# The MLP of a two-layer decoder: the norm's factor, squared, applied once to the sum of three or four down quarters instead of to every up chunk

## The chip, the cores and the metric

The kernel runs on one core of a Trainium2 chip. The metric is device time in microseconds (us) of one execution. Shapes in profile rows are partitions x elements. PE is the matrix engine (TensorE), DVE is VectorE, ACT is ScalarE, POOL is GpSimd, SP is the engine whose queue issues nearly all DMAs. DVE and ACT each work off one queue in the order in which the program stands.

## The reference

The whole program is two decoder layers on 512 tokens of width 1024, then a final norm. The change is in the MLP that ends each layer:

```python
def rmsnorm(x, g):
    xf = x.astype(jnp.float32)
    y = xf * lax.rsqrt(jnp.mean(xf * xf, axis=-1, keepdims=True) + EPS)
    return (y * g.astype(jnp.float32)).astype(x.dtype)

def hybrid_layer(...):
    ...                                   # attention, retention, gates
    x = x + mixed @ w_out
    h2 = rmsnorm(x, g_mlp)
    x = x + jnp.square(jax.nn.relu(h2 @ w_up)) @ w_down
    return x
```

`w_up` is 1024 x 4096 and `w_down` 4096 x 1024. The norm's factor is one number r for each token, and relu is positively homogeneous, so relu(r·u)² = r²·relu(u)². The factor can therefore be applied to the 4096 up channels, or, squared, to the 1024 columns that come out of `w_down`.

## The kernel before, in words

Everything lies transposed: channels on the 128 partitions, the 512 tokens along the free axis. `x` holds 8 chunks of 128 channels. All products are made in three passes to keep float32 accuracy: each operand is split into a high part (`hi`, rounded by ACT) and a low part (`lo`, the rest, by DVE), and PE adds hi·hi, hi·lo and lo·hi.

Weights stream through SP's queue, 512 KB at a time, in an order written out by hand (`unit_order`). `split_until` turns each raw unit into `hi` (ACT, L286) and `lo` (DVE, L287), three units ahead of their use; the tiles of `raw`, `hi` and `lo` have three buffers each.

The MLP works in four quarters q = 0..3 of 1024 up channels. The order is in `mlp_sequence`: first the four up chunks 0 to 3 (`group`), then pairs of up chunks, written here as pair (q, i), with i = 0..3, chunk number c = 8q + 2i; between two pairs stands a "down" step (q, i), which multiplies quarter q's up result with two column chunks of `w_down` (`two_chunks`: 48 products 512 wide). So down (q, i) and pair (q+1, i) alternate, until the last quarter's down follows in one piece: in layer 0 as a `group` of four chunks and four single ones, in layer 1 in `end`.

A pair is computed in Winograd's form: seven products of half blocks instead of eight, into three PSUM banks called `a`, `b` and `e`. The order on PE is a; e; b; a; b; e; b, four steps of k each. `narrow_pair` makes each step of three products 256 wide; `wide_pair` of one product 512 wide (both moving parts side by side) and one 256 wide, and then has to fold the two halves of a bank together. Pairs with a chunk number from `FIRST_WIDE` = 6 on are wide. Between the products the banks are handed on:

```python
ins = ... nc.scalar.activation(b, a, AF.Copy).ins       # b starts as a copy of a        (L1383)
multiply(e, part, False, form(0))
ins = nc.scalar.activation(eu, e, AF.Copy).ins          # e saved                        (L1386)
multiply(b, part, True, form(1), False)
ins = nc.scalar.activation(bu, b, AF.Copy).ins          # b saved, before b goes on      (L1390)
```

PE's next products into `b` wait for the copy from `a`, and its products with `form(2)` wait until `b` has been saved. At its end the pair's `z` is joined from the banks (L1362, L1363, L1367 to L1369), multiplied with the factor and clipped by DVE (L1409), squared by ACT (L1429) and split (L339, L340) into quarter q's moving operand.

The factor comes from `rms_mlp`: the squares of `x` are summed while `x` is finished (`squared_input`), and `prepare` and `finish` run inside the first up group. A down step's two banks are added to `x` by DVE (L1436). With the last quarter of layer 0, `x` also goes to DRAM (`spill`) and is split as the next layer's input; in layer 1 the two halves of `x` are turned from channels to tokens by way of DRAM (`turns`: `blocks`, L520 and L523), the first half during the last down steps of quarter 2.

Tile's scheduler sets the order of the instructions on each engine when the program is built, from an estimate of their times. The order is fixed from then on.

## Time and profile before

| | |
|---|---|
| three runs | 1468.44, 1469.42, 1469.47 us; median 1469.42 |
| profiled execution, first to last instruction | 1467.5 us (1.9 less than the median: what lies around the span) |
| PE busy | 1461.0 us, 100% |
| DVE busy | 1161.6 us, 79% |
| ACT busy | 814.6 us, 56% |
| moved by DMA | 198.65 MB, 135 GB/s on average |

The profile has one row for each kind of instruction, with the number of times it ran, its busy time and the mean of one. A row of the timeline has start, duration, engine, line, what is written and read, and, in brackets, how long the engine had been idle and who ended that. Two neighbours on one engine overlap a little, so durations add up to somewhat more than the time between starts.

### The profile page before, as it was taken

The numbers are of one execution on the slowest core, as the hardware profiler recorded it, in microseconds if no ns is written. First come the engines' busy times: TensorE is split into PE (matmuls) and PEld (weight loads), VectorE is DVE, ScalarE is ACT, GpSimd is POOL, SyncE is SP. The second block draws the span as 40 slices with busy tenths as digits, with TensorE's granted clock in tenths as the row PEclk, the third lists the DMA queues.
The fourth block names the chain that finished last, engine by engine and source line by source line (L and its number), as shares of the span: only waits on it lengthen the run. The fifth ranks groups of instructions, "written<-read, shape, count | busy, mean of one in ns | idle before, by whom it ended". The sixth has DMA issues, their size and how long they took to land.

```text
span 1467.5 us, 20166 instructions
## 1 busy us (share of the span) xinstructions
PE 1461.0 (100%) x7434; PEld 1246.4 (85%) x7434; DVE 1161.6 (79%) x1912; ACT 814.6 (56%) x1306; POOL 3.7 (0%) x14
## 2 busy tenths in 40 slices
PE   9999999999999999999999999999999999999998
PEld 7888888888988888888888888888989888888887
DVE  7998778678988787776678977786899877877774
ACT  7657356654684445444456653666547754455544
POOL 0000000000000000000000000000000000000000
PEclk9999999999999999999999999999999999999999
DMA  6423843356443332333543258323654432333373
GB/s 227 134 87 101 280 166 98 104 171 210 130 120 125 101 115 88 107 108 115 165 121 102 86 168 285 107 95 107 191 197 123 144 101 87 125 105 101 108 200 108
DMA packets 73346, 198.65 MB, mean 135 GB/s; under 512 B 8712, under 2 KB 8864, under 8 KB 73248
## 3 DMA queue, kind: packets, MB, share of 16 engines
q1 hardware_dynamic: 72960, 196.84, 42.5%
q8 instruction: 58, 0.95, 0.3%
q10 hardware_dynamic: 288, 0.52, 0.1%
q14 instruction: 40, 0.33, 0.1%
HBM read 173.73 MB, written 20.98 MB: 133 GB/s over the span
## 4 chain that ended last, share of the span: by engine, by line
PE 99%; DVE 0%; issue 0%; POOLq 0%; ACT 0%; DVEq 0%; ACTq 0%
PE mm L334 24%; PE mm L332 23%; PE mm L333 23%; PE mm L1356 11%; PE mm L1357 6%; PE rv L332 2%; PE rv L334 2%; PE rv L333 2%; PE score L864 1%; PE r L332 1%; PE r L334 1%; PE r L333 1%; PE pT L819 0%; PE pv L846 0%; PE pv L845 0%; PE warm L311 0%
## 5 line engine op out<-in xcount | busy, mean ns | idle before, releaser
L333 PE MATMUL mm<-r,hi 128*128 128x512 f32 (+1 forms) x1568 | 572.5, 367 | 0.0
L332 PE MATMUL mm<-r,hi 128*128 128x512 f32 (+1 forms) x1568 | 569.9, 367 | 0.0
L334 PE MATMUL mm<-r,lo 128*128 128x512 f32 (+1 forms) x1568 | 563.9, 367 | 0.2
L286 ACT ACTIVATE hi<-raw 128x1024 fp32r<-128x1024 f32 (+1 forms) x334 | 333.9, 1002 | 377.8 <-PE mm L333 206.9
L287 DVE TENSOR_TENSOR lo<-raw,hi 128x512 fp32r<-128x512 f32 (+1 forms) x335 | 384.3, 1150 | 110.8 <-ACT hi L286 109.4
L334 PEld LDWEIGHTS mm<-r,lo 128*128 128x128 f32 x1568 | 293.6, 188 | 48.8 <-DVE lo L287 1.4
L332 PEld LDWEIGHTS mm<-r,hi 128*128 128x128 f32 x1568 | 294.1, 188 | 46.5 <-ACT r L342 0.2
L333 PEld LDWEIGHTS mm<-r,hi 128*128 128x128 f32 x1568 | 294.3, 188 | 46.0
L1356 PE MATMUL mm<-r,hi 128*128 128x512 f32 x728 | 252.0, 391 | 0.0
L1357 PE MATMUL mm<-r,lo 128*128 128x256 f32 x728 | 200.3, 277 | 0.0
L1356 PEld LDWEIGHTS mm<-r,hi 128*128 128x128 f32 x728 | 136.5, 188 | 28.7 <-ACT mm L1383 0.2
L1357 PEld LDWEIGHTS mm<-r,lo 128*128 128x128 f32 x728 | 136.7, 188 | 3.2 <-DVE lo L287 0.6
L1429 ACT ACTIVATE z<-z 128x512 f32<-128x512 f32 x56 | 32.5, 624 | 51.8 <-DVE z L1409 51.8
L1436 DVE TENSOR_TENSOR x<-x,mm 128x512 f32<-128x512 f32 x56 | 37.7, 686 | 28.1 <-PE mm L334 28.1
L334 PE MATMUL rv<-hi,r 128*128 128x512 f32 x128 | 49.8, 389 | 0.0
L333 PE MATMUL rv<-lo,r 128*128 128x512 f32 x128 | 49.8, 389 | 0.0
L332 PE MATMUL rv<-hi,r 128*128 128x512 f32 x128 | 49.8, 390 | 0.0
L339 ACT ACTIVATE r<-z 128x512 fp32r<-128x512 f32 x64 | 38.5, 619 | 16.3 <-DVE z L1090 16.1
L340 DVE TENSOR_TENSOR r<-z,r 128x512 fp32r<-128x512 f32 x64 | 42.9, 685 | 4.7 <-ACT r L339 4.3
L891 ACT ACTIVATE sm<-sm,st 128x256 f32<-128x256 f32 (+1 forms) x64 | 30.1, 472 | 19.0 <-DVE st L879 18.8
L1409 DVE SCALAR_TENSOR_TENSOR z<-z,rstd 128x512 f32<-128x512 f32 x52 | 35.6, 685 | 0.6
L340 DVE TENSOR_TENSOR r<-sums,r 128x1024 fp32r<-128x1024 f32 x24 | 28.9, 1216 | 0.0
(270 smaller groups left out, 1679.2 us busy)
## 6 DMA issues: line engine op xcount, KB each, us to landing
raw<-w_in_in SPq DMA_DIRECT2D x89, 512.0 KB, 3.6
raw<-w_down_in SPq DMA_DIRECT2D x64, 512.0 KB, 3.6
raw<-w_up_in SPq DMA_DIRECT2D x32, 512.0 KB, 3.9
raw<-w_up_in SPq DMA_DIRECT2D x60, 256.0 KB, 2.9
raw<-w_a_in SPq DMA_DIRECT2D x8, 512.0 KB, 6.5
ahead<-w_b_in SPq DMA_DIRECT2D x8, 512.0 KB, 5.4
park_w_b<-ahead SPq DMA_DIRECT2D x16, 256.0 KB, 5.9
ahead<-w_up_in SPq DMA_DIRECT2D x8, 512.0 KB, 5.7
```

Of the source, the lines that this page charges most:

```text
L286: nc.scalar.activation(hi[:, at], raw[:, at], AF.Copy)
L287: last_low[:] = [nc.vector.tensor_tensor(lo[:, at], raw[:, at], f32(hi[:, at]), ALU.subtract).ins]
L332: nc.tensor.matmul(ps, ah, bh, start=start and i == 0, stop=False, **more)
L333: nc.tensor.matmul(ps, ah, bl, start=False, stop=False, **more)
L334: nc.tensor.matmul(ps, al, bh, start=False, stop=stop and i == n - 1, **more)
L339: nc.scalar.activation(hi, src, AF.Copy)
L340: nc.vector.tensor_tensor(lo, src, f32(hi), ALU.subtract)
L1356: nc.tensor.matmul(both, hi[:, c], m, start=start and k == 0, stop=False, **more)
L1357: nc.tensor.matmul(ps[:, :H], lo[:, c], m[:, 0, :], start=False, stop=k == 3 and start, **more)
L1409: nc.vector.scalar_tensor_tensor(z[:, :, at], z[:, :, at], 0.0, factor, ALU.max, ALU.mult)
L1429: nc.scalar.activation(z[:, i, :], z[:, i, :], AF.Square)
L1436: nc.vector.tensor_tensor(x[:, c, :], x[:, c, :], ps, ALU.add)
```

## The change

The up chunks no longer carry the factor. Each is only clipped, squared and split. The squared factor, 1/(mean + eps), is applied once to the sum of the down quarters: in layer 0 to the sum of all four (`plain` = 4), in layer 1 to the sum of the first three (`plain` = 3), after which the last quarter's pairs carry the plain factor (`root`) as before. In detail:

- Layer input: when a chunk of `x` is final after `w_out`, it is stored to DRAM (`kept`, 8 stores of 256 KB for each layer) and not squared then. The squares are taken in the first up group, in its last two steps.
- Down quarter 0 is copied into `x` by ACT (L1440). Each further quarter starts with `x` copied into its two PSUM banks by ACT (`seed`, L1429), the products are added on top of it, and the result is copied back by ACT. At the last plain quarter DVE multiplies the bank with the squared factor and adds the old `x`, which comes back from `kept` (4 loads of 512 KB for each layer, `kept_pair`).
- `FIRST_WIDE` is 4, so pair (0, 2) is wide too.
- In `wide_pair`, `b` is no longer saved to `bu` but copied into bank `e` (L1384), onto which the later products of `e` are added; the two halves of `eu` are folded once, and one add of each join falls away. Relu and square are done by ACT on 1024 elements at once, and the split too.
- `finish` of the factor comes after down (0, 0), without a square root; layer 1 takes one root for its last quarter.

```diff
-FIRST_WIDE, LAST_WIDE = 6, 32
+FIRST_WIDE, LAST_WIDE = 4, 32
...
         def next_input(c):
             scaled_input(c, g_mlp)
-            squared_input(c, g_mlp)
+            nc.sync.dma_start(kept[:, c, :], x[:, c, :])
...
             def join_copied(dest, ps, u):
-                nc.vector.tensor_tensor(u[:, :H], u[:, :H], u[:, H:], ALU.add)
-                nc.vector.tensor_tensor(u[:, :H], u[:, :H], ps[:, H:], ALU.add)
-                nc.vector.tensor_tensor(dest, ps[:, :H], u[:, :H], ALU.add)
+                side = temp("side")[:, :H]
+                nc.vector.tensor_tensor(side, ps[:, H:], u, ALU.add)
+                nc.vector.tensor_tensor(dest, ps[:, :H], side, ALU.add)
...
             multiply(b, part, True, form(1), False)
-            ins = nc.scalar.activation(bu, b, AF.Copy).ins
+            nc.vector.tensor_tensor(u, u, eu[:, H:], ALU.add)
+            ins = nc.scalar.activation(e, b, AF.Copy).ins
...
-            for half in (1, 0):
-                ...
-                nc.vector.scalar_tensor_tensor(z[:, :, at], z[:, :, at], 0.0, factor, ALU.max, ALU.mult)
+            join(z[:, 1, :H], b)
+            if q < plain:
+                nc.scalar.activation(z, z, AF.Relu)
+            else:
+                factor = roots[0].unsqueeze(1).broadcast_to([P, 2, T])
+                nc.vector.scalar_tensor_tensor(z, z, 0.0, factor, ALU.max, ALU.mult)
...
-            for i in range(2):
-                nc.scalar.activation(z[:, i, :], z[:, i, :], AF.Square)
-                split(hi[:, i, :], lo[:, i, :], z[:, i, :])
+            nc.scalar.activation(z, z, AF.Square)
+            split(hi, lo, z)
...
+        def seed(c):
+            ps = bank(ps_mm, "mm")
+            nc.scalar.activation(ps, x[:, c, :], AF.Copy)
+            return ps
+        def kept_pair(c):
+            two = big("kept")
+            nc.sync.dma_start(two, kept[:, c : c + 2, :])
+            return two
+        def put_down(c, q, old=None):
             def put(ps):
-                nc.vector.tensor_tensor(x[:, c, :], x[:, c, :], ps, ALU.add)
+                if q < plain - 1:
+                    nc.scalar.activation(x[:, c, :], ps, AF.Copy)
+                    return
+                t = temp("down")
+                nc.vector.tensor_tensor(t, ps, rms_mlp.value, ALU.mult)
+                nc.vector.tensor_tensor(x[:, c, :], t, old[:, c % 2, :], ALU.add)
...
+                old = kept_pair(2 * i) if q == plain - 1 else None
+                seeded = [seed(c) for c in (2 * i, 2 * i + 1)] if q else None
+                two_chunks("w_down", layer, up[q], [put_down(c, q, old) for c in (2 * i, 2 * i + 1)], turning, seeded)
+                if (q, i) == (0, 0):
+                    rms_mlp.finish()
```

The scheduler builds a new order from this. Counted over both layers, PE has 112 products 256 wide less and 56 products 512 wide more; ACT has 57 instructions more (40 seeds, 40 copies back, and larger ones in place of smaller), DVE 126 fewer, SP 24 DMAs more.

**ACT, where pair (1, 2) of layer 0 begins.** `z` is the pair before, (1, 1); `mm` are PSUM banks, `side` and `eu` parts of the joins, `hi<-raw` the weights. Before:

```order
L286 ACTIVATE hi<-raw_4563 128x1024
L1362 ACTIVATE side<-mm 128x256
L1429 ACTIVATE z<-z 128x512 x2
L339 ACTIVATE r_87<-z 128x512
L286 ACTIVATE hi<-raw_4658 128x1024
L339 ACTIVATE r_87<-z 128x512
L1383 ACTIVATE mm<-mm 128x512
L286 ACTIVATE hi<-raw 128x512
L1386 ACTIVATE eu<-mm 128x512
L1390 ACTIVATE bu<-mm 128x512
```

Now, in the same place (L1376 is what was L1383, L1384 what was L1390):

```order
L1359 ACTIVATE side<-mm 128x256
L1400 ACTIVATE z<-z 128x1024
L1422 ACTIVATE z<-z 128x1024
L1440 ACTIVATE x<-mm 128x512
L339 ACTIVATE r_87<-z 128x1024
L286 ACTIVATE hi<-raw_4632 128x1024
L1440 ACTIVATE x<-mm 128x512
L1376 ACTIVATE mm<-mm 128x512
L286 ACTIVATE hi<-raw 128x512
L1379 ACTIVATE eu<-mm 128x512
L1384 ACTIVATE mm<-mm 128x512
```

The copy of bank `a` to bank `b` used to stand behind squares, splits and a weight conversion alone, none of which needs the last down step. It now stands behind two copies of down banks to `x` as well, which do, and between those two stand the split of `z` and the weight conversion.

**ACT, from pair (0, 3) to down (0, 0) and pair (1, 0) of layer 0.** Here `r_89` is the high part of pair (0, 3), which down (0, 0) multiplies with, `rstd<-own` the factor's four copies. Before:

```order
L286 ACTIVATE hi<-raw_4210 128x1024
L1362 ACTIVATE side<-mm 128x256
L1383 ACTIVATE mm<-mm 128x512
L286 ACTIVATE hi<-raw_4305 128x1024
L1386 ACTIVATE eu<-mm 128x512
L1429 ACTIVATE z<-z 128x512 x2
L1390 ACTIVATE bu<-mm 128x512
L339 ACTIVATE r_89<-z 128x512
L286 ACTIVATE hi<-raw 128x512
L339 ACTIVATE r_89<-z 128x512
```

Now:

```order
L286 ACTIVATE hi<-raw_4186 128x1024
L1359 ACTIVATE side<-mm 128x256
L1400 ACTIVATE z<-z 128x1024
L1376 ACTIVATE mm<-mm 128x512
L1422 ACTIVATE z<-z 128x1024
L472 ACTIVATE rstd<-own 64x256 x4
L286 ACTIVATE hi<-raw_4288 128x1024
L1379 ACTIVATE eu<-mm 128x512
L339 ACTIVATE r_89<-z 128x1024
L286 ACTIVATE hi<-raw 128x512
L1359 ACTIVATE side<-mm 128x256
L1384 ACTIVATE mm<-mm 128x512
```

Relu and square of `z`, the four copies of the factor and a weight conversion now stand ahead of the split into `r_89`, and the bank copy L1384 stands behind that split.

**SP, at the last down step of quarter 2 in layer 1**, where half of `x` is turned. Before:

```order
L225 DMA raw<-w_up_in 128x1024
L196 DMA raw<-w_down_in 128x1024
L520 DMA blocks<-turned 128x512 x2
L523 DMA x<-blocks 32x4x512 x4
L196 DMA raw<-w_down_in 128x1024 x4
```

Now:

```order
L225 DMA raw<-w_up_in 128x1024
L196 DMA raw<-w_down_in 128x1024
L520 DMA blocks<-turned 128x512 x2
L523 DMA x<-blocks 32x4x512 x4
L1434 DMA kept<-kept 128x1024
L196 DMA raw<-w_down_in 128x1024 x4
```

The last load of the old `x` stands behind the four loads of the turned blocks, which wait for their stores.

## The prediction

> **What bounds the kernel now.** I read the page's first parts, then the chain, then who makes PE wait.

> ```profile
> span 1467.5 us, 20166 instructions
> PE 1461.0 (100%) x7434; PEld 1246.4 (85%) x7434; DVE 1161.6 (79%) x1912; ACT 814.6 (56%) x1306; POOL 3.7 (0%) x14
> PEclk9999999999999999999999999999999999999999
> PE 99%; DVE 0%; issue 0%; POOLq 0%; ACT 0%; DVEq 0%; ACTq 0%
> PE warm L311 <- DVE ones L306: 1.0, 1, 1.0
> ```

> PE is busy all the time at full clock; the chain that ended last is PE itself, and the waits of PE hold one row, at the program's start. So a microsecond that DVE saves is worth nothing unless PE waited for it, and time can change in two ways only: PE gets other products, or PE begins to wait. DVE is the fuller of the helpers (79%), ACT has 44% free. But free share is no cover by itself: PE waits for particular ACT instructions, and those for what stands ahead of them in ACT's queue. So I price the products first and then walk ACT's and SP's queue at the places shown above.

> **Products.** A row's duration overlaps its neighbour, so the price of a product is the distance of starts.

> ```profile
> 423.96 0.28 PE L332 MATMUL mm<-r,hi 128*128 128x256 f32 x1
> 430.32 0.28 PE L332 MATMUL mm<-r,hi 128*128 128x256 f32 x1
> ...
> 513.78 0.39 PE L333 MATMUL mm<-r,hi 128*128 128x512 f32 x1
> 515.36 0.39 PE L334 MATMUL mm<-r,lo 128*128 128x512 f32 x1
> 516.27 0.40 PE L1356 MATMUL mm<-r,hi 128*128 128x512 f32 x1
> 517.53 0.28 PE L1357 MATMUL mm<-r,lo 128*128 128x256 f32 x1
> 520.70 0.39 PE L1356 MATMUL mm<-r,hi 128*128 128x512 f32 x1
> ```

> Narrow: from 423.96 to 430.32 lie 54 products, 0.118 us each. Down: 513.78 to 515.36 are 7, 0.226 each. Wide: 516.27 to 520.70 are 13 couples of 512 and 256, 0.341 each. A narrow pair has 84 products, 9.89 us; a wide one 28 couples, 9.55. Pair (0, 2) going wide saves 0.34 in each layer: **−0.7 us**. The extra product that clears a bank is there once a layer before and after.

> **What the helpers are given.** These are the prices on ACT and DVE, from the groups by shape:

> ```profile
> L286 ACT ACTIVATE hi<-raw 128x1024 fp32r<-128x1024 f32 x291 | 307.3, 1057 | 364.3 <-PE mm L333 204.6 <-PE mm L1356 101.3 <-issue 26.3
> L1429 ACT ACTIVATE z<-z 128x512 f32<-128x512 f32 x56 | 32.5, 624 | 51.8 <-DVE z L1409 51.8
> L1390 ACT ACTIVATE bu<-mm 128x512 f32<-128x512 f32 x26 | 15.4, 592 | 6.0 <-PE mm L1357 6.0
> L1383 ACT ACTIVATE mm<-mm 128x512 f32<-128x512 f32 x22 | 12.8, 581 | 5.6 <-PE mm L1357 5.5
> L565 ACT ACTIVATE mm<-x 128x512 f32<-128x512 f32 x3 | 1.8, 591 | 0.6 <-DMA x<-blocks 0.6
> L1362 ACT ACTIVATE side<-mm 128x256 f32<-128x256 f32 x52 | 18.9, 364 | 0.0
> L472 ACT ACTIVATE rstd<-own 64x256 f32<-64x256 f32 x8 | 3.3, 416 | 0.8 <-DVE own L469 0.7
> L287 DVE TENSOR_TENSOR lo<-raw,hi 128x1024 fp32r<-128x1024 f32 x291 | 354.7, 1220 | 105.0 <-ACT hi L286 103.5
> L1409 DVE SCALAR_TENSOR_TENSOR z<-z,rstd 128x512 f32<-128x512 f32 x52 | 35.6, 685 | 0.6
> L1363 DVE TENSOR_TENSOR z<-mm,side 128x256 f32<-128x256 f32 x52 | 21.6, 415 | 0.0
> ```

> Relu and square of 1024 elements have no row; bounded by the 1024-wide conversion (1.06) below and two 512-wide squares (1.25) above, I take 1.06, the same engine at the same width. ACT gains 40 seeds and 40 copies back (0.59 each, 47 us), about 52 relus and squares of 1024 for 56 squares of 512 (+20), and little else: some 66 us. DVE loses about as much (two factor products of 0.69 and one add of 0.42 in each of 26 pairs, 40 adds to `x`). DVE's relief is worth at most the small waits that PE has for it, so the question is what ACT's 66 us stand in front of.

> How late is late, from this timeline:

> ```profile
> 515.79 1.37 DVE L1436 TENSOR_TENSOR x<-x,mm 128x512 f32<-128x512 f32 x2 [1.07 <-PE mm L334]
> 515.82 1.14 ACT L339 ACTIVATE uhi<-z 128x512 fp32r<-128x512 f32 x2
> 517.84 0.58 ACT L1383 ACTIVATE mm<-mm 128x512 f32<-128x512 f32 x1 [0.89 <-PE mm L1357]
> ...
> 1389.95 0.58 ACT L1383 ACTIVATE mm<-mm 128x512 f32<-128x512 f32 x1
> 1390.58 0.50 PE L1356 MATMUL mm<-r,hi 128*128 128x512 f32 x1
> ```

> A helper that waits for a 512-wide product starts 0.43 after the product's start (515.36 to 515.79), for a 256-wide one 0.31 (517.53 to 517.84). Two ACT instructions behind each other overlap by 0.1 (1.14 for two of 0.62). And the last two rows show such a wait already: the bank copy ended at 1390.53 when PE wanted it, and that product took 0.50 for 0.39. I add 0.1 from a helper's end to PE. The copy is needed 4 couples (1.37 us) after its cause, so it has 1.37 − 0.31 − 0.58 − 0.1 = 0.4 us to spare: one 1024-wide instruction in front of it is more than that.

> **A. L1376, a to b, where pairs (1, 2), (2, 2), (2, 3) and (3, 2) begin, both layers: 8 places.** The first copy to `x` starts 0.43 after its bank's last product. Then ACT has 0.59 + 1.06 (split) + 1.06 (weights) + 0.59 + 0.58 − 4 × 0.1 = 3.48. With 0.1 to PE: 4.01. PE has from that product 4 down products (0.91) and 8 couples (2.73): 3.64. Late by 0.37, bounds 0.2 and 0.5: **+3.0**.

> **B. L1384, b to e, in pairs (1, 3) and (3, 3) of layer 0 and (1, 3) of layer 1.** Two seeds, `eu` and two weight conversions now stand between L1376 and L1384: 0.31 + 0.58 + 2 × 0.59 + 0.58 + 1.06 + 0.62 + 0.58 − 0.6 + 0.1 = 4.41, against 12 couples and one product, 4.21: 0.2 each, bounds 0 and 0.4: **+0.6**.

> **C. The first pairs, both layers.** Here the first group's relus, squares and splits, pair (0, 2) and (0, 3) and the factor meet. (1) In pair (0, 3), from the last product of `a` to the need for L1384, ACT has 12 instructions, 8.4 − 1.1 = 7.3 us; PE 16 couples, two 512-wide products of the norm and one product, 6.0. The 12 are three weight conversions, four steps on up chunks, four copies of banks or parts of them and the relu of pair (0, 2). If ACT has none of them behind it, PE is 1.6 late; if the first two, 0.2. I take the middle, 0.8. (2) The split into `r_89`: from the last product of `b` DVE has two `lo`, two small operations on the mean and the join, 3.3, then ACT relu, L1376, square, four factor copies, weights, `eu`, split: 7.1 − 0.9 = 6.2; with 0.31 and 0.1: 9.9. PE has 13 down products and 16 couples until it needs the tile, 8.5: 1.4 late. (3) Two products later it needs L1384, behind weights and `side`: 0.62 + 0.36 + 0.58 − 0.2 against 0.45: 0.9 more. Together 3.1 a layer, bounds 1.8 and 3.9: **+6.2**.

> **D. Pair (3, 0) of layer 1.** Down (2, 1) begins inside it, two products after the last use of the `hi` tile that its weights go into: 0.43 + 1.06 + 0.1 − 0.45 = 1.1, and L1384 behind it 0.3 more. Bounds 0.7 and 2: **+1.4**.

> **E. The last load of old `x`, layer 1.**

> ```profile
> 1407.00 2.32 SPq L523 DMA_DIRECT2D x<-blocks  x4
> 1410.16 0.58 ACT L1383 ACTIVATE mm<-mm 128x512 f32<-128x512 f32 x1 [0.29 <-PE mm L1357]
> gate<-aside SPq DMA_DIRECT2D x8, 512.0 KB, 5.1
> raw<-w_down_in SPq DMA_DIRECT2D x64, 512.0 KB, 3.6
> x<-blocks SPq DMA_DIRECT2D x8, 256.0 KB, 5.7
> ```

> SP has the four block loads out at 1409.3; the load behind them, like `gate<-aside` 512 KB written by the kernel itself, lands 5.1 later, 1414.4. DVE's queue holds the two adds that wait for it, and behind these the `lo` of the weights: 0.69 + 0.69 + 1.22 − 0.2, ready at 1416.8. PE's last `a` product came at 1409.85 (0.31 before the copy at 1410.16) and it wants that `lo` 4.4 later, 1414.2. Late by 2.6; with 3.6 or 5.7 to landing 1.1 or 3.2: **+2.6**.

> **What costs nothing.** The other 7 loads of old `x` and the rest of the seeds: they stand 7 us of products or more ahead of their use. The 16 stores are 256 KB each beside queues that are 42% used. The longer way of the last quarter into the next layer (a product and an add for one add) is hidden by layer 1's first products, which reach chunk 7 last. The move of the squares takes DVE work out of the `w_out` pairs; PE's waits there and where the first wide pair starts are of this size:

> ```profile
> 432.08 0.40 PE L1356 MATMUL mm<-r,hi 128*128 128x512 f32 x1
> 432.48 0.39 PE L1357 MATMUL mm<-r,lo 128*128 128x256 f32 x1
> ```

> 0.40 from start to start for 0.23: 0.17. A few of these may go: **−0.3**, bounds 0 and −1.5.

> **The sum.** 3.0 + 0.6 + 6.2 + 1.4 + 2.6 − 0.7 − 0.3 = +12.8. The profiled span of 1467.5 becomes 1480.3; the median of the runs lies 1.9 above the span, so 1482.2, 0.9% slower. By the low ends +1.6 + 0 + 3.6 + 0.7 + 1.1 − 2.2 = +4.8, by the high ends +4.0 + 1.2 + 7.8 + 2.0 + 3.2 − 0.7 = +17.5.

> **Rivals.** A measurement of this kernel tells 0.2%, 3 us, from no change.

> *Everything stays hidden.* Against the walk above speaks that PE before waits nowhere though the same scheduler set that order too; if ACT on 1024 elements is shorter than I take it, or banks are free earlier, only the products count: 1469.4 − 0.7 − 0.3 = 1468.4, no change. It decides if ACT's stretch in A is below 3.1 us for my 3.5 and the one in C below 4.8 for 6.2; the 1390.58 row, where a far lighter queue is already late, speaks against it. Chance 0.08.

> *DVE's relief counts.* If all PE's hidden small gaps were DVE's (0.17 at a dozen places, 2 us) and went, with 0.7 from the products: 1466.5, just at the border of faster. The 100% of PE speaks against more. Chance 0.02.

> *PE's clock falls.* A wait of over 3 us, as E can become, could put PE back to the rate that it has at the program's start:

> ```profile
> 1.04 4.63 PE warm L311 x10
> ```

> There a 512-wide product takes 0.46 for 0.23, so 4 us at that rate cost 2: 1484 to 1485. [...] Chance 0.06.

> *SP's queue backs up.* Each `kept` store waits for a chunk of `x` on DVE, and weight loads stand behind it; four `kept` loads, 2 MB, go out among the last weights of layer 0. At 5.1 for 3.6 to landing, 1.5 us for some three units: 5 us more, 1487. Weights are asked for three units, 16 us, ahead, which speaks against it. Chance 0.12.

> **Numbers.** My forecast has 0.72; its own range is 1476 to 1488. The range given starts below its low end (1474.2), where the walk would be almost wholly hidden, and reaches to the backed-up queue, 1489. Slower: 0.72 + 0.06 + 0.12 = 0.90; no change 0.08; faster 0.02.

> **What would show it.** Right: PE's waits list ACT's L1376 and L1384 and DVE's L287 some twenty times, 0.2 to 1.5 us each; pairs from (1, 1) on keep their 9.55 and pair (0, 2) has it; ACT near 880 us busy, DVE near 1095; `kept` loads 5 us to landing, and DVE idle for DMA near the last. Wrong: a waits list with one row, or waits for `raw` or seeds (L1429), which I count as covered.

## The result, and the profile after

The changed kernel takes 1490.77 us (median of four runs, 1490.14 to 1491.0) where the kernel before takes 1469.03: a ratio of 1.0147, 95% interval 1.0133 to 1.0161. It is slower, as forecast, but by 21.7 us for the 12.8 predicted, and 1.8 us above the range. The profiled execution has a span of 1488.4, 20.9 more than before. First the page: span, busy times, granted clock, and the chain by engine.

```profile
span 1488.4 us, 20035 instructions
PE 1468.8 (99%) x7378; PEld 1245.9 (84%) x7378; DVE 1105.7 (74%) x1786; ACT 880.1 (59%) x1363; POOL 3.7 (0%) x14
PEclk9999999999999999999999999999999999999999
PE 90%; ACT 5%; DVE 2%; DMA 2%; issue 1%; POOLq 0%; SPq 0%; ACTq 0%; DVEq 0%
```

The helpers' work came out as counted: ACT 880.1 us (near 880 was predicted), DVE 1105.7 (near 1095). And yet the chain is no longer PE's alone: 9% of it now belongs to ACT, DVE and DMA. The chain enters them where PE waits, and follows their work from there back, so this share is larger than the waits themselves. The list of these had one row before and has nine now (what PE ran, for whom it waited; total, times, longest):

```profile
PE mm L332 <- ACT r L339: 4.1, 2, 2.1
PE mm L1354 <- DVE lo L287: 2.9, 1, 2.9
PE mm L1353 <- ACT mm L1384: 1.5, 4, 0.5
PE mm L1353 <- ACT mm L1376: 1.1, 1, 1.1
PE warm L311 <- DVE ones L306: 1.0, 1, 1.0
PE mm L332 <- ACT hi L286: 0.9, 1, 0.9
PE mm L333 <- DVE r L340: 0.6, 1, 0.6
PE mm L334 <- DVE lo L287: 0.6, 2, 0.3
PE mm L1353 <- ACT hi L286: 0.3, 1, 0.3
```

The list drops short waits (L1376 stands in it once, and occurs eight times), so the waits are taken from the timeline below: distance from one PE start to the next, less the price of the product (0.23 us for 512 columns, 0.12 for 256). Summed by the terms of the prediction, over the whole profiled execution:

| term | predicted | measured | where |
|---|---|---|---|
| A, L1376 where pairs begin | 3.0 | 3.3 | seven of 0.29 to 0.30; pair (3, 2) of layer 1 1.23 |
| B, L1384 in pairs (1, 3), (3, 3) | 0.6 | 0.8 | 0.24, 0.33, 0.25 |
| C, first pairs, both layers | 6.2 | 7.7 | 0.8 + 2.2 + 0.8 in each; the last is for L1384 in layer 0, but for L340 in layer 1 |
| D, down (2, 1) in pair (3, 0), layer 1 | 1.4 | 1.3 | 1.08 + 0.21 |
| E, last load of old `x` | 2.6 | 3.7 | 0.49 for L286, then 3.2 for L287 |
| half clock behind long waits | 0 (a rival: 2) | 2.6 | twice, 1.2 and 1.3 |
| products, removed waits, all else | −1.0 | +1.5 | see below |
| sum | 12.8 | 20.9 | |

The row before the sum adds up from five things. The products save 0.5. Waits that the kernel before had and that went, or grew, make −0.8. The program's start took 0.3 more in this execution. The first product behind a wait takes 0.34 us from its start to the next one's, for 0.23: that is about 0.11 at each of the 23 waits above 0.2 us, some 2.0 beyond what the terms above hold and what the kernel before had. The last 0.5 is spread over thousands of products and was not traced.

**C**, first pairs, layer 0: PE, ACT and DVE around down (0, 0) and pair (1, 0).

```profile
453.08 0.42 DVE L1360 TENSOR_TENSOR z<-mm,side 128x256 f32<-128x256 f32 x1
453.54 1.06 ACT L1400 ACTIVATE z<-z 128x1024 f32<-128x1024 f32 x1 [2.60 <-DVE z L1360]
...
455.97 1.68 ACT L472 ACTIVATE rstd<-own 64x256 f32<-64x256 f32 x4
457.67 1.06 ACT L286 ACTIVATE hi<-raw 128x1024 fp32r<-128x1024 f32 x1
457.87 0.28 PE L1354 MATMUL mm<-r,lo 128*128 128x256 f32 x1
...
459.11 1.05 ACT L339 ACTIVATE r<-z 128x1024 fp32r<-128x1024 f32 x1
460.21 0.97 PE L332 MATMUL mm<-r,hi 128*128 128x512 f32 x2 [2.06 <-ACT r L339]
460.84 0.60 ACT L1384 ACTIVATE mm<-mm 128x512 f32<-128x512 f32 x1
```

PE's last product before down (0, 0) goes on starts at 457.87 and takes 0.12; the next starts at 460.21, since the split into `r_89` ended at 460.16: 2.2 us late. ACT is busy without a break from 453.54, and what is between the relu and the split is what the order showed.

**A**, where pair (1, 2) of layer 0 begins:

```profile
500.04 0.60 ACT L1440 ACTIVATE x<-mm 128x512 f32<-128x512 f32 x1
500.54 1.05 ACT L339 ACTIVATE r<-z 128x1024 fp32r<-128x1024 f32 x1
501.49 1.05 ACT L286 ACTIVATE hi<-raw 128x1024 fp32r<-128x1024 f32 x1
502.44 0.58 ACT L1440 ACTIVATE x<-mm 128x512 f32<-128x512 f32 x1
502.91 0.60 ACT L1376 ACTIVATE mm<-mm 128x512 f32<-128x512 f32 x1
503.14 0.28 PE L1354 MATMUL mm<-r,lo 128*128 128x256 f32 x1
503.56 0.50 PE L1353 MATMUL mm<-r,hi 128*128 128x512 f32 x1
503.90 0.28 PE L1354 MATMUL mm<-r,lo 128*128 128x256 f32 x1
```

The five instructions of the step stand back to back, 500.04 to 503.51, 3.47 us for the 3.48 of the working; PE's next product starts 0.42 after the last one's start, for 0.12, and then takes 0.34 to the following start, for 0.23: the piece behind a wait.

**E**, layer 1, SP's load of old `x` and who waits for it:

```profile
1424.92 0.42 SPq L1434 DMA_DIRECT2D kept<-kept  x1
1429.62 0.28 PE L1354 MATMUL mm<-r,lo 128*128 128x256 f32 x1
1430.23 0.73 PE L1353 MATMUL mm<-r,hi 128*128 128x512 f32 x2 [0.33 <-ACT hi L286]
1431.42 1.29 DVE L1444 TENSOR_TENSOR x<-down,kept 128x512 f32<-128x512 f32 x2 [2.73 <-DMA kept<-kept]
1432.63 2.96 DVE L287 TENSOR_TENSOR lo<-raw,hi 128x1024 fp32r<-128x1024 f32 x3
1433.90 0.58 PE L1354 MATMUL mm<-r,lo 128*128 128x256 f32 x1 [2.94 <-DVE lo L287]
```

DVE can use the load 6.5 us after its issue; it idles 2.73 us for it, the two adds and the `lo` of the weights follow, and PE waits for that `lo`.

**The clock.** The windows at the three longest waits (length, then busy time of each engine; the third number from the right is the granted clock):

```profile
457.11:460.52 3.41, 1.35 (x8) 0.94 (x7) 1.76 (x3) 3.37 (x6) 0.00 (x0) 1.00 0.00 0
460.52:463.93 3.41, 3.10 (x9) 2.13 (x8) 1.88 (x3) 0.92 (x3) 0.00 (x0) 0.50 0.23 67
463.93:467.34 3.41, 3.41 (x19) 2.86 (x18) 2.39 (x5) 1.12 (x2) 0.00 (x0) 1.00 0.03 10
1190.97:1194.38 3.41, 2.34 (x14) 1.82 (x12) 0.45 (x1) 3.35 (x8) 0.00 (x0) 1.00 0.00 0
1194.38:1197.79 3.41, 1.84 (x7) 1.23 (x8) 2.24 (x3) 3.38 (x5) 0.00 (x0) 1.00 0.00 0
1429.91:1433.32 3.41, 0.73 (x2) 0.30 (x2) 1.90 (x3) 2.00 (x4) 0.00 (x0) 1.00 0.47 189
1433.32:1436.73 3.41, 2.83 (x9) 2.54 (x10) 2.89 (x5) 0.00 (x0) 0.00 (x0) 0.50 0.37 96
1436.73:1440.14 3.41, 3.41 (x18) 2.82 (x18) 2.77 (x6) 1.06 (x1) 0.00 (x0) 1.00 0.66 211
```

After C's wait in layer 0 and after E's, PE ran at half clock for exactly 3.41 us. After the same wait of C in layer 1 (2.2 us, around 1194) it did not. The page's row of nines doesn't show this: a slice there is 37 us long.

### The profile page after: what moved, and what is told of

It reads as the page before. It is cut to its first block, busy times and chain, and to the rows that moved or that the text cites. A ratio compares the mean times of both kernels' runs of the same rounds, so it can differ in the third digit from the quotient of the medians.

```text
span 1488.4 us, 20035 instructions
## 1 busy us (share of the span) xinstructions
PE 1468.8 (99%) x7378; PEld 1245.9 (84%) x7378; DVE 1105.7 (74%) x1786; ACT 880.1 (59%) x1363; POOL 3.7 (0%) x14
## 4 chain that ended last, share of the span: by engine, by line
PE 90%; ACT 5%; DVE 2%; DMA 2%; issue 1%; POOLq 0%; SPq 0%; ACTq 0%; DVEq 0%
PE mm L334 22%; PE mm L333 22%; PE mm L332 22%; PE mm L1353 9%; PE mm L1354 4%; PE rv L332 2%; PE rv L333 2%; PE rv L334 2%; ACT hi L286 1%; DMA raw<-w_up_in 1%; DVE lo L287 1%; PE score L864 1%; ACT x L1440 1%; ACT r L339 1%; PE r L332 1%
## 5 line engine op out<-in xcount | busy, mean ns | idle before, releaser
L332 PE MATMUL mm<-r,hi 128*128 128x512 f32 (+1 forms) x1512 | 556.7, 371 | 5.0 <-ACT r L339 4.1
L333 PE MATMUL mm<-r,hi 128*128 128x512 f32 (+1 forms) x1512 | 557.2, 370 | 0.6 <-DVE r L340 0.6
L334 PE MATMUL mm<-r,lo 128*128 128x512 f32 (+1 forms) x1512 | 548.0, 370 | 0.6 <-DVE lo L287 0.6
L286 ACT ACTIVATE hi<-raw 128x1024 fp32r<-128x1024 f32 (+1 forms) x334 | 333.9, 1002 | 337.5 <-PE mm L333 187.3
L287 DVE TENSOR_TENSOR lo<-raw,hi 128x512 fp32r<-128x512 f32 (+1 forms) x335 | 384.3, 1151 | 147.2 <-ACT hi L286 142.8
L332 PEld LDWEIGHTS mm<-r,hi 128*128 128x128 f32 x1512 | 283.8, 188 | 53.0 <-ACT r L339 4.7
L334 PEld LDWEIGHTS mm<-r,lo 128*128 128x128 f32 x1512 | 282.8, 188 | 48.6 <-DVE lo L287 1.4
L333 PEld LDWEIGHTS mm<-r,hi 128*128 128x128 f32 x1512 | 283.9, 188 | 46.1 <-DVE r L340 1.0
L1353 PE MATMUL mm<-r,hi 128*128 128x512 f32 x784 | 276.4, 396 | 4.1 <-ACT mm L1384 1.5
L1354 PE MATMUL mm<-r,lo 128*128 128x256 f32 x784 | 217.5, 279 | 2.9 <-DVE lo L287 2.9
L1353 PEld LDWEIGHTS mm<-r,hi 128*128 128x128 f32 x784 | 148.0, 189 | 40.8 <-ACT mm L1376 4.5
L340 DVE TENSOR_TENSOR r<-z,r 128x1024 fp32r<-128x1024 f32 (+1 forms) x40 | 40.3, 1007 | 44.3 <-ACT r L339 44.3
L334 PE MATMUL rv<-hi,r 128*128 128x512 f32 x128 | 49.8, 389 | 0.0
L333 PE MATMUL rv<-lo,r 128*128 128x512 f32 x128 | 49.8, 389 | 0.0
L332 PE MATMUL rv<-hi,r 128*128 128x512 f32 x128 | 49.8, 390 | 0.0
L339 ACT ACTIVATE r<-z 128x1024 fp32r<-128x1024 f32 (+1 forms) x40 | 35.3, 884 | 16.5 <-DVE z L1090 16.1
L1400 ACT ACTIVATE z<-z 128x1024 f32<-128x1024 f32 x24 | 25.5, 1063 | 27.3 <-DVE z L1360 27.3
L1422 ACT ACTIVATE z<-z 128x1024 f32<-128x1024 f32 x28 | 29.7, 1060 | 14.0 <-DVE z L1403 13.4
L252 DVE TENSOR_TENSOR raw<-raw 128x512 f32<-128x512 f32 x28 | 19.3, 691 | 23.0 <-DMA raw<-w_up_in 23.0
L340 DVE TENSOR_TENSOR r<-sums,r 128x1024 fp32r<-128x1024 f32 x24 | 29.1, 1219 | 0.0
## 6 DMA issues: line engine op xcount, KB each, us to landing
raw<-w_in_in SPq DMA_DIRECT2D x89, 512.0 KB, 3.6
raw<-w_down_in SPq DMA_DIRECT2D x64, 512.0 KB, 3.6
raw<-w_up_in SPq DMA_DIRECT2D x32, 512.0 KB, 3.7
raw<-w_up_in SPq DMA_DIRECT2D x60, 256.0 KB, 2.9
raw<-w_a_in SPq DMA_DIRECT2D x8, 512.0 KB, 7.6
ahead<-w_b_in SPq DMA_DIRECT2D x8, 512.0 KB, 6.5
park_w_b<-ahead SPq DMA_DIRECT2D x16, 256.0 KB, 4.5
ahead<-w_up_in SPq DMA_DIRECT2D x8, 512.0 KB, 4.2
```

What stands on the lines that cost most here:

```text
L286: nc.scalar.activation(hi[:, at], raw[:, at], AF.Copy)
L287: last_low[:] = [nc.vector.tensor_tensor(lo[:, at], raw[:, at], f32(hi[:, at]), ALU.subtract).ins]
L332: nc.tensor.matmul(ps, ah, bh, start=start and i == 0, stop=False, **more)
L333: nc.tensor.matmul(ps, ah, bl, start=False, stop=False, **more)
L334: nc.tensor.matmul(ps, al, bh, start=False, stop=stop and i == n - 1, **more)
L339: nc.scalar.activation(hi, src, AF.Copy)
```

## The experiments

The theory: all of the loss is PE's waits at these places, set by what stands ahead in the queues of ACT, DVE and SP, and the clock behind the longest of them. Rivals: it is the amount of ACT's work, or adding on in PSUM with its copies, or the traffic of `kept`. Unless it says otherwise, a kernel is the changed one with one edit; times are medians, "waits" are sums over PE's timeline as above (33.1 us in the changed kernel, 2.6 of it half clock; 12.1 before).

**The load of old `x` ahead of the block loads** (term E)

```diff
-        turning = []
+        turning, olds_ahead = [], {}
...
-                old = kept_pair(2 * i) if q == plain - 1 else None
+                if q == plain - 1:
+                    for j in (i, i + 1) if i == 2 else (i,) if i < 2 else ():
+                        olds_ahead[j] = kept_pair(2 * j)
+                old = olds_ahead.pop(i) if q == plain - 1 else None
```

> Only change to the changed kernel: in the last plain quarter the loads of old x for down (2,2) and (2,3) are both issued with down (2,2), so in layer 1 the last of them stands ahead of the four block loads on SP and not behind them. Theory (PE waits at single places for what stands ahead in a queue): the waits of 0.5 and 3.2 us near 1430 shrink to about 0.4 and 0.8, and the half clock behind them (1.4 us) goes: 1490.8 - 2.4 - 1.4 = 1487.0. If the clock falls for another reason than that wait: 1488.4. Rival 1: the two adds on DVE and the weights' lo behind them are late by themselves, not the load: 1490.8. Rival 2: the gain is not at single places but DMA traffic (8 MB more) slows everything: no change either, and PE's waits elsewhere stay spread.

Measured: 1485.39 us, ratio 1.0115 (1.0101 to 1.0128), 1.6 below the expectation. The 3.2 us wait for `lo` has become:

```profile
PE mm L1354 <- DVE lo L287: 0.5, 1, 0.5
1427.40 0.73 PE L1353 MATMUL mm<-r,hi 128*128 128x512 f32 x2 [0.34 <-ACT hi L286]
```

The waits at E fell from 3.7 to 1.3 us, as expected, and the wait for L1376 in pair (3, 2) of layer 1 shrank from 1.23 to 0.43. The queue's order was the cause. The four runs of this kernel spread from 1483.61 to 1488.94, and the clock goes with them: a mean of 0.999, 0.998, 0.998 and 0.996 from the shortest to the longest. The profiled one, the shortest, has no stretch of half clock before its end, though both of C's waits of 2.2 us are there.

**Relu, square and split in halves** (lumps or amount)

```diff
-                nc.scalar.activation(z, z, AF.Relu)
+                for i in range(2):
+                    nc.scalar.activation(z[:, i, :], z[:, i, :], AF.Relu)
...
-            nc.scalar.activation(z, z, AF.Square)
-            split(hi, lo, z)
+            for i in range(2):
+                nc.scalar.activation(z[:, i, :], z[:, i, :], AF.Square)
+                split(hi[:, i, :], lo[:, i, :], z[:, i, :])
```

> Only change: relu, square and split of a pair's z are done in two halves of 512, not in one piece of 1024. ACT's work grows (about 14 us by 0.18 us for each of some 78 pieces), but no piece ahead of a bank copy is longer than 0.6 us. Theory (a long piece ahead of the copy that PE waits for): the waits for L1376 where pairs begin (3.3 us in all) and for L1384 in pairs (1,3), (3,3) (0.8) go, since those copies can be set ahead of half the work; at the first pairs the order is new, by a walk over the new order 1.9 and 0.4 in pair (0,3) of both layers and 1.9 in pair (1,0) of layer 1; all waits together 4 us less: 1486.8, or 1485.8 if the half clock in layer 0 goes with the 2.2 us wait there. Rival (the amount of ACT's work decides): PE's waits for ACT grow: 1491 to 1493.

Measured: 1486.17, ratio 1.0119 (1.0105 to 1.0133). The page's line of busy times:

```profile
PE 1467.3 (99%) x7378; PEld 1247.0 (84%) x7378; DVE 1105.1 (74%) x1814; ACT 896.1 (60%) x1443; POOL 3.7 (0%) x14
```

ACT has 16 us more to do and PE waits less: 30.7 us, of which 5.0 are half clock (three stretches), so 25.7 for 30.5 of true waits. The waits of A are gone at seven of eight places, B's all; new ones stand where the walk had put them (1.7 for 1.9 in pair (0, 3) of both layers, 2.7 for 1.9 in pair (1, 0) of layer 1), and one, for L1376 in pair (3, 1) of layer 1, is 2.0 where the expectation has none. So the amount of ACT's work is not what decides.

**Relu and square as one DVE instruction**

```diff
-                nc.scalar.activation(z, z, AF.Relu)
+                pass
...
-            nc.scalar.activation(z, z, AF.Square)
+            if q < plain:
+                nc.vector.scalar_tensor_tensor(z, z, 0.0, z, ALU.max, ALU.mult)
+            else:
+                nc.scalar.activation(z, z, AF.Square)
```

> Only change: in the plain quarters relu and square of z are one DVE instruction, max(z,0)*z, 1024 wide, in place of two on ACT. ACT loses about 51 us of work (48 x 1.06), DVE gains about 31 (24 x some 1.3; 1137 us, still below the 1162 of the kernel before). Theory (what stands ahead of PE's instruction on ACT): waits for L1376 go (3.3 us), C shrinks from about 9 to 3 (0.5 in layer 0, 2.3 in layer 1, no half clock in layer 0), waits for L1384 in pairs (1,3), (3,3) become 0.4 each for 0.25 to 0.33, down (2,1) in pair (3,0) of layer 1 and the last load of old x stay: about 8 us less, 1482.5. Rival (DVE was what the change relieved, and giving work back makes PE wait for DVE): L287 and L340 on DVE take the place of the ACT rows in PE's waits, 1489 to 1493.

Measured: 1484.82, ratio 1.0107 (1.0092 to 1.0123); 2.3 us short of the expected gain. The true waits fell by 6.5 us to 24.0, but two stretches of half clock, each double (6.83 us), took 6.0 (2.6 in the changed kernel). And three waits are longer than walked: 1.75 us for 0.5 at the split into `r_89` in layer 0, 1.46 for none at L1376 in pair (3, 2) of layer 1, and, in layer 1, the split into the tile of down (0, 0), 3.2 for 2.3:

```profile
1186.93 1.28 ACT L1488 ACT_TABLE_LOAD   x1
1188.22 0.63 ACT L1488 ACTIVATE root<-rstd 128x512 f32<-128x512 f32 x1
1188.76 1.04 ACT L339 ACTIVATE r<-z 128x1024 fp32r<-128x1024 f32 x1
1189.85 1.22 PE L332 MATMUL mm<-r,hi 128*128 128x512 f32 x2 [3.00 <-ACT r L339]
```

The new order had put layer 1's root ahead of the split, and with it a load of ACT's function table, 1.28 us; whether the walk had priced it is not on record. In layer 0 DVE's reciprocal for the factor (L469, 1.75 us) now stands ahead of the pair's last join, so the work moved to DVE comes late there. No row of PE's waits names DVE at a place where it did not stand before: the rival's sign is missing.

**The wide first pair alone, on the kernel before**

```diff
-FIRST_WIDE, LAST_WIDE = 6, 32
+FIRST_WIDE, LAST_WIDE = 4, 32
...
-            z = wide_pair(c == FIRST_WIDE + 2, ...
+            z = wide_pair(c == FIRST_WIDE, ...
```

> The kernel before with one part of the change alone: FIRST_WIDE = 4, so that pair (0,2) of both layers is computed wide. Products: 0.34 us less in each layer. Theory (the first pairs leave the helpers too little room): by a walk over the new order PE waits 1.4 us for a lo (L287) in pair (0,2) itself, 1.2 for hi (L286) at a down step in pair (0,3) and 0.3 one pair later, in each layer: 2 x 2.9 - 0.7 = 5 more, 1474.2. Rival (products count, helpers keep up as in all later wide pairs): 1468.3.

Measured: 1475.02, ratio 1.004 (1.0028 to 1.0053). This part alone, which saves 0.3 us of products a layer, makes the kernel before 6.0 us slower:

```profile
PE mm L1357 <- DVE lo L287: 3.2, 2, 1.6
PE mm L332 <- ACT hi L286: 2.1, 2, 1.0
```

So a wide pair that starts while DVE and ACT still have the first group's work leaves them too little time for its own weights: 1.8 us of wait in pair (0, 2), 1.2 in pair (0, 3) and 0.3 one pair later in each layer, for the 1.4, 1.2 and 0.3 of the walk. What this part costs inside the changed kernel, with the other causes there, was not run.

**The factor one down step later** (term C)

```diff
-                if (q, i) == (0, 0):
+                if (q, i) == (1, 0):
                     rms_mlp.finish()
```

> Only change to the changed kernel: the factor is finished after down (1,0) and not after down (0,0), so DVE's and ACT's steps on it (four copies of 0.42 us on ACT among them) leave the place ahead of the split into r_89. Theory: the waits of 2.2 and 0.8 us in both layers where down (0,0) ends go, and the half clock behind them, about 7 us; L1384 in pair (0,3) is late 1.3 for 0.8 in both layers, since ACT's order there is new, and the factor's steps bring 1.4 us of new waits in each layer near pair (1,3) and down (1,1) (L339 0.3, L340 1.0, L1376 0.2): 1490.8 - 7 + 1 + 2.8 = 1487.5. Rival (ACT is late there by its amount of work, not by the factor's steps): the 2.2 us wait stays, 1490 to 1491.

Measured: 1489.59, ratio 1.0132 (1.0117 to 1.0148), 2.1 above the expectation. The wait of 2.2 us and the 0.8 behind it are gone in both layers, so the factor's steps were what stood ahead. But L1384 in pair (0, 3) is 1.3 late, as expected, and the factor is in the way at its new place too, near down (1, 1): 2.3 us a layer where 1.4 were expected. E's wait brought a double stretch of half clock in this execution, 3.0 us.

**No seeds** (adding on in PSUM undone; term A)

```diff
-                seeded = [seed(c) for c in (2 * i, 2 * i + 1)] if q else None
+                seeded = None
```

with DVE adding `x` again in `put_down`, and the seeds of layer 0's last quarter gone too.

> Only change: down steps start with an empty bank, as before the change, and DVE adds x (quarters 1 and 2) instead of ACT copying x into the bank and back. ACT loses 40 seeds and 24 copies back or so, DVE gains as many adds. Theory: of the waits for L1376 (3.3 us at 8 places) those that stand behind copies back go; by a walk over the new order pair (1,2) of both layers (0.3 each) and pair (3,2) of layer 1 (0.3 to 1.2) keep theirs, the first pairs, down (2,1) in pair (3,0) and the last load of old x stay as they are: 1490.8 - 2 = 1488.8. Rival (adding on in PSUM, with its seeds and copies, is what costs): the loss of 21.7 us is for the most part gone, 1470 to 1476.

Measured: 1491.33 (1489.82 to 1492.82), ratio 1.0148 (1.0134 to 1.0162). It is 2.5 above the expectation. The waits for L1376 went at the places named (pair (3, 2) of layer 1 kept 1.7, where 0.3 to 1.2 were expected), and true waits fell by 1.9 us, for the expected 2, to 28.6. The profiled execution has three stretches of half clock, 4.1 us, for two and 2.6, which takes most of that back; no gain is left in the time. That adding on in PSUM is most of the cost is refuted.

**All causes taken away, pair (0, 2) narrow**: early load, later factor, relu and square on DVE and split in halves, `FIRST_WIDE` = 6.

> The changed kernel with each named cause taken away and the new algebra kept: old x loaded early, factor finished after down (1,0), relu and square as one DVE instruction in halves of 512, split in halves, and pair (0,2) narrow (clipped by DVE). Seeds in PSUM, one factor for the sum of quarters and the 24 more DMAs stay. Theory (the loss is waits at those places and nothing else): by a walk over the new order PE's waits are 0.8 us above those of the kernel before, in pair (0,2) and (0,3) of both layers 0.4 for L287 and 0.6 at the last units, no half clock: 1470, between 1469 and 1472. Rival (8 MB more through DMA, or ACT's total, costs by itself): 1475 or more.

Measured: 1472.12, ratio 1.0018 (1.0010 to 1.0027), 0.1 above the expected range. Of the 21.7 us, 2.8 are left, with the algebra, the seeds and all 24 DMAs in place. PE's waits in it, apart from the program's start:

```profile
PE mm L1356 <- ACT mm L1387: 0.8, 2, 0.4
PE mm L1356 <- ACT mm L1379: 0.7, 1, 0.7
PE mm L334 <- DVE lo L287: 0.6, 2, 0.3
PE mm L1357 <- DVE lo L287: 0.4, 2, 0.2
```

The sum of waits is 15.3 for 12.1, so 3.2 more where 0.8 were walked. That traffic, or the amount of ACT's work, is the cost is refuted: it had put 1475 or more, with all the traffic still there. The kernel is still slower than before: what the change saves elsewhere, PE never waited for.

**The same with pair (0, 2) wide**

> The same as the run with all causes taken away, but pair (0,2) stays wide. Theory: products 0.7 us less, and PE waits 1.3 us for hi (L286) at a down step in pair (0,3) of both layers: 1.8 more than with the narrow pair, 1471.5 in all. Rival (the wide first pair is the gain of 0.7 once ACT has room): 1469.3.

Measured: 1472.83, ratio 1.0023 (1.0014 to 1.0032). The waits for L286 are there as walked, 1.3 us in each layer, and cost more than the 0.7 that the products save. The two intervals overlap, so that narrow is better here is likely, not shown. No version that was run beats the kernel before.

**Waits made on purpose, on the kernel before**: the bank copy from `a` to `b` repeated in 22 pairs.

```diff
+        stalls = [0]
...
+            stalls[0] += 1
+            for _ in range(0 if close else (1, 2, 3, 4)[stalls[0] % 4]):
+                nc.scalar.activation(b, a, AF.Copy)
             ins = nc.vector.tensor_copy(b, a).ins if close else nc.scalar.activation(b, a, AF.Copy).ins
```

> The kernel before, with the bank copy from a to b in most wide pairs done 2 to 5 times over instead of once, so that PE waits for the last of them: waits of about 0.8 to 2.9 us in 22 pairs, well apart, on a kernel whose clock otherwise never falls. Question: from which wait on does PE's clock fall. Rule 1 (a wait must reach a fixed length of about 3 us): no clock fall here at all; time 1469 + 43 = 1512. Rule 2 (a clock that looks at fixed stretches of some 3.3 us, which run on their own, and falls when most of one was idle): waits of 1.7 to 2.9 us bring half clock in some pairs and not in others of the same wait, each fall lasts some 3.3 us and costs up to 1.7; waits below 1.5 none: 2 to 8 falls, 1515 to 1525.

Measured, in one run: 1515.55, and one fall of the clock. PE waits 44 us more than before, 43 by the expectation. Two waits are the longest, 2.8 us each, one in pair (1, 0) of either layer: the clock fell after the one of layer 0 and not after the other. Rule 1's "none" and rule 2's "two to eight" both missed; what decides is in the windows before and at the fall, and in the two windows that came nearest to one:

```profile
455.76:459.17 3.41, 0.79 (x5) 0.56 (x4) 1.65 (x2) 3.41 (x7) 0.00 (x0) 1.00 0.00 0
459.17:462.58 3.41, 3.41 (x12) 2.72 (x11) 1.29 (x2) 1.38 (x3) 0.00 (x0) 0.50 0.00 0
...
483.06:486.48 3.42, 1.58 (x10) 1.15 (x8) 2.32 (x3) 3.42 (x8) 0.00 (x0) 1.00 0.00 0
1234.00:1237.41 3.41, 1.56 (x10) 1.13 (x8) 2.31 (x4) 3.41 (x8) 0.00 (x0) 1.00 0.00 0
```

The same with (6, 7, 8, 10) in place of (1, 2, 3, 4):

> The same with 7 to 11 copies: waits of about 2.4 to 4.3 us, often two in one pair. Rule 1: falls after waits over 3 to 3.4 us alone. Rule 2: falls after nearly all waits over 2.7, some of two stretches (6.6 us) where the wait fills more than one.

Measured, in one run: 1614.97, a mean clock of 0.971 and 19 falls, of one or two stretches. Rule 2 holds in kind; where its line lies is told in the last section.

## Why the prediction was right and wrong

Right: that PE waits at single places and where. All of A to E are in the trace at the places named, A's stretch of ACT to 0.01 us, and with the engine and line named but for two waits (L340 in layer 1's C, L286 in E). Undoing a cause removed its waits: E, the factor's part of C, and A each by its own run; D was never undone by itself. "Everything stays hidden" and "DVE's relief counts" are refuted: DVE lost 56 us, and the small waits that went are worth 0.8. SP's queue didn't back up: no wait of PE for `raw` weights is in the list.

Partly luck: A's sum. Seven places measured 0.30 for the 0.37 of the working, and the eighth 1.23, of which 0.8 belong to the late load of old `x`. The first part of C, 0.8, was the middle of two bounds and not walked.

Wrong, by step; the prediction failed by the size of its terms and by two that it left out:

- **C(2), the split into `r_89`**: predicted 1.4 late, 2.2 in both layers. DVE's chain from `b` to the join took 3.7 us for 3.3 (453.50 is its end), and ACT's from relu to split 6.6 for 6.2 (453.54 to 460.16): four factor copies take 1.68 back to back, where 0.1 had been taken off for each neighbour. C measured 7.7 for 6.2. Part (3), 0.9 for L1384, was that in layer 0 alone; in layer 1 PE waited for the low part of the split (L340).
- **E**: landing was taken as 5.1 us, from the nearest row of the same size; it was 6.4, and both high end (3.2) and forecast (2.6) lay below the 3.7 measured. The load stood behind four block loads, of which one at least was still moving: it landed at 1427.75. Why it took longer is not shown: other loads of old `x`, with no block load ahead of them, landed 4.8 to 8.5 us after issue.
- **The clock**: the prediction had a rival for it, chance 0.06, and let it come after a "wait of over 3 us", so at E alone. It fell at E and after C's 2.2 us wait in layer 0: 2.6 us. The sum had nothing for it, and the condition, a wait of over 3 us, does not hold.
- **The products' −0.7, the removed waits' −0.3, and nothing else**: the products are there (−0.5), and so are the removed waits (−0.8). What the sum lacks is the piece behind each wait, 0.11 us, 2.0 in all. The prediction's row at 1390.58 shows it, 0.50 for 0.39, and was used only to price the time from a helper's end to PE's start. The wide first pair was counted as a gain of 0.7; on the kernel before, it alone costs 6.0.

Without the clock the sum would be 18.3, 1488 by the time of the runs: inside the range, but above the 17.5 of the prediction's own high ends. Of the 8.1 us that the sum is short, C and E are 2.6, the clock 2.6, and the row of small things 2.5.

## What to carry to other kernels

Here, with the matrix engine at 100%, time that the change took off another engine was worth next to nothing (56 us of DVE, 0.8 us of PE's waits), and what it moved could only cost. So walk the queue of each helper at the places where the matrix engine takes its result, with nothing taken off for overlap where the trace shows none, add the piece behind each wait, here 0.11 us, and give a load's landing time the spread that the trace shows, here 4.8 to 8.5 us. Price each part of a change that comes in several parts by itself: here the one that was to save 0.7 us cost 6.0 by itself. And price the half clock behind a long wait: here a wait of 2.2 us brought 1.2 to 1.3 us of it in one layer and none in the other.

## What the runs showed of the hardware

The clock's rise at the program's start lay on the same grid: in the changed kernel full clock came 6.55 us after the start, 133.0 steps ahead of the first fall. In the kernel before, whose first products are the same, it came after 5.80 us. So the grid lay differently in these two executions.

Take PE's idle time (starts less prices) in each step of the grid. In the changed kernel and the runs with short and with long waits, all 22 steps ahead of a fall had 2.15 us or more of it, and of the other steps at full clock none had more than 2.16. The two nearest are both in the run with long waits: 2.15 in the step from 1422.98, after which the clock fell, and 2.16 in the one from 1395.67, after which it stayed. So what decided a fall in these three executions was whether about 2.15 of the 3.41 us of one step, 63%, were idle, and not the length of a wait: C's 2.2 us lay inside one step in layer 0 (2.3 idle, the clock fell) and across two in layer 1 (1.2 and 2.0, it stayed). Whether a second step at half clock followed went by idle time too: in the run with long waits PE idled 0.8 us of the step at most in the 11 falls of one step (with each product priced double), and 0.86 us or more of the first step in the 8 falls of two.

The grid fits the spread of the runs: the kernel with the early load, with waits of 2.2 us, spreads over 5 us, the kernel before, with none, over less than 2. It is not shown to be all of it, for only one execution of each kernel was profiled: without seeds two runs at a mean clock of 0.995 took 1489.82 and 1492.82.

In a step at half clock a 512-wide product took 0.43 us from start to start, for 0.23 at full clock. A step of it cost 1.2 and 1.3 us in the changed kernel, and 1.6 in the run with short waits, where PE worked through all of it.

So an edit's time and its waits can differ: without seeds PE waits 1.9 us less in the profiled execution, with one fall more, and the median is 0.6 us longer.
